# The gates of the recurrence as 64-row products on two halves of the array, two tiles at a time

## The chip, the core and the metric

The kernel runs on one core of one Trainium2 chip. Its time is the device time of one execution in microseconds (us); lower is better. Times are medians over executions, and a profile is one execution taken by the hardware profiler. Engines in it: PE (TensorE: matrix products; PEld is its weight load, shown apart), ACT (ScalarE: functions of one operand), DVE (VectorE: element work on two operands), POOL (GpSimd) and SP (SyncE, which here only issues DMAs). Products write into PSUM, eight banks of 128 partitions x 512 f32 elements; everything else is in SBUF or in device memory.

## What is computed

One layer of a decoder over 512 tokens of width 1024: a normalisation, one combined projection, three token mixers side by side (a gated chunk mixer, block-sparse attention, a recurrence), their gated sum, an output projection, and a SwiGLU block. The change lies in the recurrence:

```python
xc = lax.conv_general_dilated(xr, conv_w[:, None, :], window_strides=(1,), padding=[(CONV_WIDTH - 1, 0)],
                              dimension_numbers=('NWC', 'WIO', 'NWC'), feature_group_count=RNN_WIDTH) + conv_b
xh = xc.reshape(B, S, RNN_HEADS, RNN_HEAD_DIM)                       # 16 heads of 64
r = sigmoid(einsum('bshi,hio->bsho', xh, w_a).reshape(B, S, RNN_WIDTH) + b_a)
i = sigmoid(einsum('bshi,hio->bsho', xh, w_x).reshape(B, S, RNN_WIDTH) + b_x)
log_a = -LRU_C * r * softplus(-lam)
a = exp(log_a)
b_in = sqrt(-expm1(2.0 * log_a)) * (i * xc)
h_t = a_t * h_(t-1) + b_in_t                                         # over the 512 tokens
y_c = h * gelu(gate)
```

Each of the 16 heads has its own 64x64 matrix for each of the two gates, r and i.

## The kernel before

**Arithmetic.** Every f32 product is made of three in a faster form: an operand is split into a high part (an ACT copy, `hi`) and a low part (a DVE subtraction, `lo`) by `split` (L131, L136), and hi·hi, hi·lo and lo·hi are added up in one PSUM bank.

**Tiles.** Work goes by tiles of 128 output columns x 512 tokens. `matrix` (L269, products at L263) makes one with 24 products: eight blocks of the inner dimension, three each. Before it `unit` (L252) takes weights that are already split, and has the weights two tiles ahead loaded (SP) and split; loaded weights have two buffers, split ones three. In this stage PSUM has six banks for tag `mm` and two for tag `tr` (L72).

**The recurrence.** Its 1024 channels are eight tiles (`xr_tile`, L488), in two batches of four; a tile holds two heads, one on partitions 0 to 63, one on 64 to 127. A tile does this: 24 products; the convolution out of the bank (one ACT instruction, L499, and three DVE ones, L501) into `xc`; the split of `xc` into `ch` and `cl`; a pause; then the gates. For each gate there is a 128x128 weight matrix with the two heads' matrices on its diagonal and zeros elsewhere, three products of 128 rows (L509: hi·ch, hi·cl, lo·ch) into a bank of tag `tr`, and one ACT instruction that evicts it: a sigmoid into `R` (L511), or a tanh into `TI` (L514), which DVE multiplies by `xc` (L515). The gate weights are split early, during the first stage, by `load_wab` (L464).

`rec_batch` (L518) then takes a whole batch: tanh of `R` (L523), a square root of all four tiles (L524, for which ACT loads another table), exponentials (L530, yet another table), two DVE products and the scan over tokens. `rg_tile` (L545) makes the other factor, `rec_out` (L551) multiplies and splits the results, `yc_sums` (L567) forms sums of them (the first at L577) that the branch's products (L1273) read.

**Order.** Tiles are Python generators. `run` (L2049) walks through a list of them, one step at a time, a step being about six products. A tile that yields a number w is put on a list of late tiles and its remaining part is resumed after w steps of the tiles that follow, one part per step; what is left at the end of a pass is run out there. Beside the main list a side generator is advanced at a given rate per step. Three passes matter here: the first four `xr_tile`s and a small tile (`gate_tile`: 16 products, then four 64-row transposes, L722, of what a sigmoid at L718 gave); then four `rg_tile`s, a `cmp_tile` and the second four `xr_tile`s, with `rec_batch(0)` beside them at rate 0.45; then more tiles, with `both_out` (L2128: recurrence of batch 1, outputs of both) beside them, also at 0.45.

The order in which the code issues instructions is a priority. A planner with modelled costs then lays out each engine's queue at build time and draws a ready instruction ahead of an earlier one that it thinks is not ready; `issue_after` forbids that for a pair. On the chip every engine works through its queue in order and waits on semaphores.

Of the kernel before, what the change touches and what calls it, by code (L numbers as in the profile page):

```python
# [25 lines left out]
F32R = mybir.dt.float32r  # L26
I32 = mybir.dt.int32
AF = mybir.ActivationFunctionType
OP = mybir.AluOpType
# [4 lines left out]
NK = 8  # L34
# [9 lines left out]
V_CW, V_CB, V_BA, V_BX, V_LAM = 48, 80, 88, 96, 104  # L44
# [8 lines left out]
def hybrid_block(ctx: ExitStack, tc: tile.TileContext, A, out):  # L53
    nc = tc.nc
    V, SC, GP, PE, SY = nc.vector, nc.scalar, nc.gpsimd, nc.tensor, nc.sync
# [42 lines left out]
    def nm(s):  # L98
        cnt[0] += 1
        return f"{s}_{cnt[0]}"  # L100

    def slab(name, dt=F32, tag=None, shape=(4, S), first=0):
        pool, bufs = (merge if tag == "m" else big, TAGS[tag]) if tag in TAGS else phase_pool[tag]
        if tag not in ("y", "mo", "f", "wab"):
            return pool.tile([128, *shape], dt, tag=tag, name=nm(name), bufs=bufs)
        size = 2064 if tag == "f" else 2112
        t = pool.tile([128, size], dt, tag=tag, name=nm(name), bufs=bufs)[:, first:first + math.prod(shape)]
        return t if len(shape) == 1 else t.rearrange(
            "p (a b) -> p a b" if len(shape) == 2 else "p (a b c) -> p a b c", **dict(zip("abc", shape)))

    def row(name, dt=F32, tag="row", first=0):
        bufs = {"row": 6, "q32": 2, "tg": 2}[tag]
        return mid.tile([128, S if tag == "row" else S + 32], dt, tag=tag, name=nm(name), bufs=bufs)[:, first:first + S]

    def bank(tag):
        return psum[1].tile([128, S], F32, tag=tag, name=nm(tag), bufs=psum[2][tag])
# [10 lines left out]
    def f32(ap):  # L127
        return ap.bitcast(F32)

    def split(src, hi, lo, lo_eng=None):  # L130
        res["hi"] = SC.activation(hi, src, AF.Copy)  # L131
        e = lo_eng or V
        if e is GP:
            GP.tensor_sub(lo, src, f32(hi))
        else:
            res["lo"] = V.tensor_sub(lo, src, f32(hi))  # L136

    res = {}
# [138 lines left out]
    def const0(shape, name):  # L277
        return phase_pool["s0"][0].tile(shape, F32, name=name, bufs=1)
# [7 lines left out]
    vec = const0([128, NVEC], "vec")  # L286
# [3 lines left out]
    half = const0([128, 3, 8], "half")  # L290
# [164 lines left out]


    wab = {}

    def start_wab():
        wab["raw"] = slab("wabr", tag="s1", shape=(2, NK, 128))  # L460
# [2 lines left out]

    def load_wab():  # L464
        raw = wab["raw"]
        hi = slab("wabh", F32R, "wab", (2, NK, 128), 48)
        lo = slab("wabl", F32R, "wab", (2, NK, 128), 48)
        wab["hi"], wab["lo"] = hi, lo
        for _ in range(4):
            yield  # L470
        for k in range(0, NK, 2):
            split(raw[:, :, k:k + 2], hi[:, :, k:k + 2], lo[:, :, k:k + 2])
            yield

    yc = {}
    rec = {}
# [11 lines left out]
    def xr_tile(b, c):  # L488
        if c == 0:
            res["late"] = res["raw"]  # L490
            rec[b] = dict(R=slab("r", tag="y" if b else "m"), GG=slab("gg", tag="m"), TI=slab("ti", tag=("s0", "s1")[b]))
        k = 4 * b + c
        ps = bank("mm")
        yield from matrix(ps, hh, hl)
        xc = row("xc")

        def cw(w):
            return vec[:, V_CW + 8 * w + k:V_CW + 8 * w + k + 1]
        res["xc"] = SC.activation(xc, ps, AF.Identity, scale=cw(3), bias=vec[:, V_CB + k:V_CB + k + 1])  # L499
        for i in (1, 2, 3):  # L500
            res["cv"] = V.scalar_tensor_tensor(xc[:, i:], ps[:, :S - i], cw(3 - i), xc[:, i:], op0=OP.mult, op1=OP.add)  # L501
        yield
        ch, cl = row("ch", F32R), row("cl", F32R)
        split(xc, ch, cl)
        yield 4
        for g, dst in ((0, "R"), (1, "TI")):
            pg = bank("tr")
            for t, (w, x) in enumerate((("hi", ch), ("hi", cl), ("lo", ch))):
                PE.matmul(pg, wab[w][:, g, k, :], x, start=(t == 0), stop=(t == 2))  # L509
            if g == 0:  # L510
                SC.activation(rec[b]["R"][:, c, :], pg, AF.Sigmoid, bias=vec[:, V_BA + k:V_BA + k + 1])  # L511
            else:
                ti = rec[b]["TI"][:, c, :]
                last = SC.activation(ti, pg, AF.Tanh, scale=0.5, bias=half[:, 0, k:k + 1])  # L514
                res["ti"] = last, V.scalar_tensor_tensor(ti, ti, 1.0, xc, op0=OP.add, op1=OP.mult)  # L515
            yield

    def rec_batch(b):  # L518
        r = rec[b]
# [180 lines left out]
    gates = shared.tile([128, 4, 64], F32, name="gates")  # L700
# [6 lines left out]
    def gate_tile():  # L707
        ps = bank("mm")
        w, _ = unit()
        for k in range(NK):  # L710
            for t, x in enumerate((hh, hl)):
                PE.matmul(ps, w[:, k * 128:k * 128 + 128], x[k], start=(k == t == 0), stop=(k == NK - 1 and t == 1))
            if k % 4 == 3:
                yield
        s = row("gsig")
        SC.activation(s[:64], ps[64:], AF.Copy)
        V.tensor_add(s[:64], s[:64], ps[:64])
        SC.activation(s[:64], s[:64], AF.Sigmoid)  # L718
        yield
        pt = bank("tr")  # L720
        for c in range(4):
            PE.transpose(pt[:, c * 64:(c + 1) * 64], s[:64, c * 128:(c + 1) * 128], ident[:64, :64])  # L722
        V.tensor_copy(gates.rearrange("p c h -> p (c h)"), pt[:, :256])
        V.tensor_scalar(gates[:, 0, 0:48:3], gates[:, 0, 0:48:3], seen, None, op0=OP.mult)
        yield

    def cmp_tile(i):
        kv, pr = divmod(i, 2)
        if i == 0:
            x = slab("xcmp", tag="xc", shape=(2, G, 8, 32))  # L730
            comp[0], comp[1] = x[:, 0], x[:, 1]
        X = comp[kv]
        ps = bank("mm")
        yield from matrix(ps, *((gh, gl) if i == 0 else (hh, hl)))

        def half_of(x, g):
            return x[g * 64:(g + 1) * 64].rearrange("p (m r e) -> p m r e", r=8, e=2)

        src = [half_of(ps, g) for g in range(2)]
        dst = [X[:, 2 * pr + g].rearrange("p r m -> p m r") for g in range(2)]  # L740
        for g in range(2):
            if i == 0:
                r = half_of(rbs, g)
                V.tensor_mul(dst[g][0:64], src[g][:, :, :, 0], r[:, :, :, 0])
                V.tensor_mul(dst[g][64:128], src[g][:, :, :, 1], r[:, :, :, 1])
            else:
                res["x0"] = SC.activation(dst[g][0:64], src[g][:, :, :, 0], AF.Copy)
        if i:
            for g in range(2):
                V.tensor_copy(dst[g][64:128], src[g][:, :, :, 1])  # L750
        yield
# [1294 lines left out]
            close(0, 3, 2 - n, part)  # L2046


    def run(main, side=None, rate=1.0):  # L2049


        credit = 0.0
        late = []
        for m in main:
            for w in m:
                for x in late:
                    x[0] -= 1
                if late and late[0][0] <= 0:
                    if next(late[0][1], 0) == 0:
                        late.pop(0)  # L2060
                if w:
                    late.append([w, m])
                    break
                credit += rate
                while side is not None and credit >= 1.0:
                    credit -= 1.0
                    if next(side, 0) == 0:
                        side = None
            credit += rate
        for _, m in late:  # L2070
            for _ in m:
                pass
        if side is not None:
            for _ in side:
                pass

    def seq(*gens):
        for g in gens:
# [19 lines left out]
    def four(tile, b):  # L2098
        return [tile(b, c) for c in range(4)]
# [10 lines left out]
    def xr_tiles(b, nxt):  # L2110

        tiles = four(xr_tile, b) + [nxt]
        return tiles[:1] + [behind(t, "xc", "cv") for t in tiles[1:]]
# [4 lines left out]
    def branch(b, y, j0=0, j1=8):  # L2118
# [3 lines left out]
        return r  # L2122

    run([v_half(0), v_half(1), cmp_tile(0)], seq(norm(), load_wab()))
    run(xr_tiles(0, gate_tile()))
    tiles = xr_tiles(1, rg_tile(1, 0))
    run(four(rg_tile, 0) + [cmp_tile(1)] + tiles[:4], rec_batch(0), 0.45)
    def both_out():  # L2128

        batch = rec_batch(1)  # L2130
        next(batch)
        yield
        yield from after(res["ti"], rec_out(0))
        yield from batch
        yield from rec_out(1)

    def inputs(tile, kv):

        for w in tile:
# [4 lines left out]

    run([tiles[4], *(rg_tile(1, c) for c in range(1, 4)), cmp_tile(2), inputs(cmp_tile(3), 0),
         behind(c_gate(0), "x0", "x1"), hidden(first), inputs(c_gate(1), 1)],
        both_out(), 0.45)
    c_stage(first)
    run([u_tile(j) for j in range(8)])
    next_phase(1)  # L2150
# [115 lines left out]
```

## Time and profile before

| | |
|---|---|
| time, median of 3 (lowest to highest) | 1090.08 us (1089.75 to 1090.09) |
| the profiled execution: its time, its span | 1089.44 us, 1087.7 us |
| clock granted to PE in it | 0.998 of full |
| gate products (L509) | 48, in the stretch from 66.8 to 146.0 us |
| evictions of gates on ACT (L511 and L514) | 16, 0.68 us each |
| table loads on ACT between 50 and 215 us | 6, 1.28 us each |

How to read the views: the page gives busy time by engine as a share of the span, and the chain of work that ended last, followed back from the last instruction to what released it at each step. The same chain can be listed in order of time (start, length, engine, bank's tag, line, count). Groups of instructions are listed by line, with busy time and mean length of one, then the idle time of the engine before them and who ended it. The timeline lists instructions in order of time (start, length, engine, line, operation, output<-inputs, the array's rows*columns that a product uses, its shape, count; several merged instructions have one length in all). A product's own length is a latency: products are pipelined, and what one costs in a stream is the distance between two starts. The table by stretches gives, for each, the busy us (and number) of PE, PEld, DVE, ACT and POOL, then the granted clock, the DMA engines' busy share and GB/s.

### The profile page before, as it was taken

Reading aid. Unit: us, or ns where it says so; the run is one execution under the profiler, and the core shown is the slowest. Engines: PE = TensorE matmul, PEld = TensorE weight load, DVE = VectorE, ACT = ScalarE, POOL = GpSimd, SP = SyncE. Lnnn points to the kernel's source line nnn. Section 1 sums busy time; section 2 is a strip of 40 time slices with the busy share of each in tenths; the row PEclk is TensorE's granted clock in tenths of the full one; section 3 lists DMA queues with packets and bytes.
Section 4 is the critical chain, followed back from the end, with each engine's and each line's share of the span. In section 5 each row is a group of like instructions: output and inputs, shape, how many; then the busy total and the mean of one; then the engine's idle time right before and its main releaser. Section 6 shows DMA issues by size and latency. Waiting matters only on the chain.

```text
span 1087.7 us, 16765 instructions
## 1 busy us (share of the span) xinstructions
PE 1078.3 (99%) x6450; PEld 948.5 (87%) x6450; DVE 883.0 (81%) x1557; ACT 661.7 (61%) x1210; POOL 29.0 (3%) x41
## 2 busy tenths in 40 slices
PE   9999999999999999999999999999999999999997
PEld 7888888999889888898888889988999999998886
DVE  6967779669675899998998887876988888889675
ACT  6757574454444676876777655555666666667542
POOL 0000000000000000000000000000000000022200
PEclk9999999999999999999999999999999999999999
DMA  8332325430322221102111134271323322378902
GB/s 312 113 99 82 97 86 204 178 98 20 117 78 78 78 59 39 59 20 79 59 39 59 58 118 136 72 257 39 117 78 117 117 104 97 130 227 202 191 20 97
DMA packets 35312, 115.07 MB, mean 106 GB/s; under 512 B 3584, under 2 KB 3984, under 8 KB 34336
## 3 DMA queue, kind: packets, MB, share of 16 engines
q1 hardware_dynamic: 28496, 97.01, 27.0%
q0 software_dynamic: 5152, 11.09, 5.0%
q10 hardware_dynamic: 1584, 5.90, 1.4%
q8 instruction: 50, 0.82, 0.3%
q14 instruction: 30, 0.25, 0.1%
HBM read 111.89 MB, written 2.10 MB: 105 GB/s over the span
## 4 chain that ended last, share of the span: by engine, by line
PE 97%; DVE 1%; DMA 0%; issue 0%; ACT 0%; DVEq 0%; SPq 0%; ACTq 0%
PE mm L263 37%; PE mm L1755 18%; PE mm L1273 7%; PE mm L1894 6%; PE mm L625 4%; PE mm L1509 4%; PE o L992 4%; PE sc L954 3%; PE tr L979 3%; PE tr L1894 3%; PE mm L870 2%; PE tr L784 1%; PE tr L509 1%; PE mm L1611 1%; PE tr L685 1%; PE tr L892 1%
## 5 line engine op out<-in xcount | busy, mean ns | idle before, releaser
L263 PE MATMUL mm<-hh,hi 128*128 128x512 f32 x504 | 199.5, 396 | 0.0
L263 PE MATMUL mm<-hh,lo 128*128 128x512 f32 x504 | 197.4, 392 | 0.0
L263 PE MATMUL mm<-hl,hi 128*128 128x512 f32 x504 | 196.9, 391 | 0.0
L136 DVE TENSOR_TENSOR lo<-raw,hi 128x1024 fp32r<-128x1024 f32 (+1 forms) x105 | 121.0, 1153 | 38.4 <-ACT hi L131 35.3
L131 ACT ACTIVATE hi<-raw 128x1024 fp32r<-128x1024 f32 (+1 forms) x105 | 105.3, 1003 | 46.5 <-PE mm L263 17.3
L263 PEld LDWEIGHTS mm<-hh,lo 128*128 128x128 f32 x504 | 94.6, 188 | 19.7
L263 PEld LDWEIGHTS mm<-hl,hi 128*128 128x128 f32 x504 | 94.7, 188 | 18.4 <-issue 0.2
L263 PEld LDWEIGHTS mm<-hh,hi 128*128 128x128 f32 x504 | 94.7, 188 | 18.0 <-PE mm L1273 0.2
L960 ACT ACTIVATE P<-P,ast 128x128 f32<-128x128 f32 (+3 forms) x128 | 70.7, 555 | 23.1 <-DVE ast L958 22.5
L958 DVE CUSTOM_DVE_ANT_0 P<-sc,mask 128x128 f32<-128x128 f32 (+3 forms) x128 | 57.9, 484 | 8.2 <-PE sc L954 7.3
L131 ACT ACTIVATE ph<-tr 128x512 fp32r<-128x512 f32 x80 | 46.9, 592 | 25.9 <-PE tr L979 24.0
L136 DVE TENSOR_TENSOR pl<-tr,ph 128x512 fp32r<-128x512 f32 x80 | 54.4, 685 | 2.7 <-PE o L992 0.9
L954 PE MATMUL sc<-K,q 128*128 128x512 f32 (+2 forms) x192 | 51.0, 368 | 0.0
L1755 PE MATMUL mm<-t,hi 128*128 128x256 f32 x288 | 50.7, 276 | 0.0
L1894 PE MATMUL mm<-hi,u 128*128 128x512 f32 x160 | 50.1, 389 | 0.0
L979 PE MATMUL tr<-ident,P 128*128 128x128 f32 x320 | 48.7, 273 | 0.0
L979 PEld LDWEIGHTS tr<-ident,P 128*128 128x128 f32 x320 | 39.0, 140 | 9.8 <-DVE pl L136 1.0
L136 DVE TENSOR_TENSOR lo<-bs,hi 128x1024 fp32r<-128x1024 f32 x28 | 34.1, 1220 | 11.6 <-ACT hi L131 11.6
L1755 PEld LDWEIGHTS mm<-t,hi 128*128 128x128 f32 x288 | 43.4, 188 | 0.0
L1755 PE MATMUL mm<-fh,hi 128*128 128x256 f32 x144 | 40.0, 278 | 0.0
L1755 PE MATMUL mm<-fh,lo 128*128 128x256 f32 x144 | 39.8, 276 | 0.0
L1755 PE MATMUL mm<-fl,hi 128*128 128x256 f32 x144 | 39.8, 276 | 0.0
(489 smaller groups left out, 2896.6 us busy)
## 6 DMA issues: line engine op xcount, KB each, us to landing
raw<-in_w_in SPq DMA_DIRECT2D x64, 512.0 KB, 3.5
rawp<-in_w_fi SPq DMA_DIRECT2D x20, 1024.0 KB, 5.1
bs<-in_w_fo POOLq DMA_DIRECT2D x20, 512.0 KB, 8.1
raw<-in_w_br SPq DMA_DIRECT2D x14, 512.0 KB, 3.6
w<-in_cw ACTq DMA_DIRECT2D x4, 1024.0 KB, 6.7
raw<-in_w_o SPq DMA_DIRECT2D x8, 512.0 KB, 4.1
bs<-in_w_fo SPq DMA_DIRECT2D x8, 512.0 KB, 8.0
raw<-in_w_v SPq DMA_DIRECT2D x6, 512.0 KB, 4.9
```

The lines of the kernel that those rows point to most:

```text
L131: res["hi"] = SC.activation(hi, src, AF.Copy)
L136: res["lo"] = V.tensor_sub(lo, src, f32(hi))
L263: res["mm"] = PE.matmul(ps[:m, n0:n1], w[:, k * 128:k * 128 + m], x[k][:, n0:n1], start=(t == 0), stop=(t == 3 * NK - 1))
L625: res["mm"] = PE.matmul(b[c], x[k][:, c * 128:(c + 1) * 128], w[:, kk * 512:kk * 512 + 512], start=(k == 0 and t == 0), stop=(k == NK - 1 ...
L954: PE.matmul(ps[:, :w * n].rearrange("p (b n) -> p b n", b=w), lhs, K[:, i, brs[0]:brs[-1] + 1, :n], start=(i == 0), stop=(i == 1))
L958: V.tensor_tensor_reduce(out=t, in0=ps[:, b * n:b * n + n], in1=mask[0][:, S - n:], scale=-0.125, scalar=3.0e38, op0=OP.add, op1=OP.min, a ...
L960: SC.activation(t, t, AF.Exp, scale=-1.0, bias=st[:, 0, j, b:b + 1], accum_out=st[:, 1, j, b:b + 1])
L979: PE.transpose(pt[:, j * 128:(j + 1) * 128], self.part(j, br)[:, kt * 128:(kt + 1) * 128], ident)
L992: PE.matmul(po, VV[:, kt, g % 2, br].rearrange("p i d -> p (i d)"), x, start=(br == 0 and kt == 0 and t == 0), stop=(br == 1 and kt == a a ...
L1273: res["mm"] = PE.matmul(ps, u[:, k * 128:k * 128 + 128], v[:, k], start=(start and k == t == 0), stop=(k == 3 and t == 2), skip_group_chec ...
L1755: res["mm"] = PE.matmul(ps, w[:, k * 128:k * 128 + 128], x[:, k], start=(start and k == t == 0), stop=(k == 3 and t == 2), skip_group_chec ...
L1894: PE.matmul(ps, a, b, start=id(ps) not in begun, stop=i == len(ops) - 1, skip_group_check=True)
```

## The change

- The gate weights are laid out by head: each half of the partitions holds its head's 64 rows, with the two gates' 64 columns side by side (`load_wab`).
- A tile's gate work is no longer done alone. The even tile of a pair is only noted; when the odd one's pause has passed, both are done as a group: four banks of tag `mm` (one for each tile and head), and twelve products of 64 rows and 128 columns, alternating between the two halves, in the order hi·ch, lo·ch, hi·cl, the odd tile ahead of the even one in each. All but the first are tied to the one before by `issue_after`.
- A bank now holds one head's two gates, the first on its partitions 0 to 63, the second on 64 to 127. So each tile has four evictions of 64 partitions instead of two of 128.
- `ch` and `cl` use the buffers of tags `tg` and `q32` (two each) instead of `row` (six).
- The pause is 3 steps instead of 4, and for the last tile of a batch 6 (batch 0) or 4 (batch 1). `run` can hand its list of late tiles on to the next pass (`keep`, `late`), so each batch's second group falls into the pass behind it. The side generators wait, a step at a time, until the batch's two groups are laid out.

```diff
-        hi = slab("wabh", F32R, "wab", (2, NK, 128), 48)
-        lo = slab("wabl", F32R, "wab", (2, NK, 128), 48)
+        hi = slab("wabh", F32R, "wab", (NK, 128), 48)
+        lo = slab("wabl", F32R, "wab", (NK, 128), 48)
...
-        for k in range(0, NK, 2):
-            split(raw[:, :, k:k + 2], hi[:, :, k:k + 2], lo[:, :, k:k + 2])
-            yield
+        for o in ends:
+            for i in range(2):
+                g = slice(64 * i, 64 * i + 64)
+                split(raw[o, i, :, o], hi[o, :, g], lo[o, :, g])
+                yield
...
-        ch, cl = row("ch", F32R), row("cl", F32R)
+        ch, cl = row("ch", F32R, "tg"), row("cl", F32R, "q32")
         split(xc, ch, cl)
-        yield 4
-        for g, dst in ((0, "R"), (1, "TI")):
-            pg = bank("tr")
-            for t, (w, x) in enumerate((("hi", ch), ("hi", cl), ("lo", ch))):
-                PE.matmul(pg, wab[w][:, g, k, :], x, start=(t == 0), stop=(t == 2))
-            if g == 0:
-                SC.activation(rec[b]["R"][:, c, :], pg, AF.Sigmoid, bias=vec[:, V_BA + k:V_BA + k + 1])
-            else:
-                ti = rec[b]["TI"][:, c, :]
-                last = SC.activation(ti, pg, AF.Tanh, scale=0.5, bias=half[:, 0, k:k + 1])
-                res["ti"] = last, V.scalar_tensor_tensor(ti, ti, 1.0, xc, op0=OP.add, op1=OP.mult)
-            yield
+        rec[b]["x"] = rec[b].get("x", []) + [(k, xc, ch, cl)]
+        yield (6 - 2 * b) if c == 3 else 3
+        if c % 2 == 0:
+            return
+        two = rec[b].pop("x")
+        pg = [[bank("mm") for _ in ends] for _ in two]
+        for t in range(3):
+            for i, (k, xc, ch, cl) in reversed([*enumerate(two)]):
+                w, x = (("hi", ch), ("lo", ch), ("hi", cl))[t]
+                for n, own in enumerate(ends):
+                    with tc.issue_after(res["gate"].ins) if t or n or not i else nullcontext():
+                        res["gate"] = PE.matmul(pg[i][n], wab[w][own, k, :], x[own], start=(t == 0), stop=(t == 2))
+        yield
+        for i, (k, xc, ch, cl) in enumerate(two):
+            R, ti = (rec[b][n][:, k % 4, :] for n in ("R", "TI"))
+            for n, own in enumerate(ends):
+                SC.activation(R[own], pg[i][n][:64], AF.Sigmoid, bias=vec[own, V_BA + k:V_BA + k + 1])
+                last = SC.activation(ti[own], pg[i][n][64:], AF.Tanh, scale=0.5, bias=half[own, 0, k:k + 1])
+            res["ti"] = last, V.scalar_tensor_tensor(ti, ti, 1.0, xc, op0=OP.add, op1=OP.mult)
+            yield
+        rec[b]["gates"] += 1
...
-    def run(main, side=None, rate=1.0):
+    def run(main, side=None, rate=1.0, late=None, keep=False):
...
-    run(xr_tiles(0, gate_tile()))
+    late = run(xr_tiles(0, gate_tile()), keep=True)
...
+    def gated(b):
+        while rec[b]["gates"] < 2:
+            yield
+        yield from rec_batch(b)
+
+    late = run(four(rg_tile, 0) + [cmp_tile(1)] + tiles[:4], gated(0), 0.45, late, True)
     def both_out():
+        while rec[1]["gates"] < 2:
+            yield
         batch = rec_batch(1)
```

`ends` is `slice(0, 64), slice(64, 128)`; `rec[b]["gates"]` starts at 0.

More of the change, by code (lines that the diff above doesn't have):

```diff
@@ L457, in hybrid_block @@
     wab = {}
+    ends = slice(0, 64), slice(64, 128)
     def start_wab():
@@ L490, in xr_tile @@
             res["late"] = res["raw"]
-            rec[b] = dict(R=slab("r", tag="y" if b else "m"), GG=slab("gg", tag="m"), TI=slab("ti", tag=("s0", "s1")[b]))
+            rec[b] = dict(gates=0, R=slab("r", tag="y" if b else "m"), GG=slab("gg", tag="m"), TI=slab("ti", tag=("s0", "s1")[b]))
         k = 4 * b + c
@@ L2046, in down @@
             close(0, 3, 2 - n, part)
-    def run(main, side=None, rate=1.0):
+    def run(main, side=None, rate=1.0, late=None, keep=False):
         credit = 0.0
-        late = []
+        late = late or []
         for m in main:
@@ L2069, in run @@
             credit += rate
-        for _, m in late:
-            for _ in m:
+        while late and not keep:
+            for _ in late.pop(0)[1]:
                 pass
@@ L2075, in run @@
                 pass
+        return late
     def seq(*gens):
@@ L2124, in hybrid_block @@
     run([v_half(0), v_half(1), cmp_tile(0)], seq(norm(), load_wab()))
-    run(xr_tiles(0, gate_tile()))
+    late = run(xr_tiles(0, gate_tile()), keep=True)
     tiles = xr_tiles(1, rg_tile(1, 0))
-    run(four(rg_tile, 0) + [cmp_tile(1)] + tiles[:4], rec_batch(0), 0.45)
+    def gated(b):
[3 more added lines that the diff above has]
+    late = run(four(rg_tile, 0) + [cmp_tile(1)] + tiles[:4], gated(0), 0.45, late, True)
     def both_out():
+        while rec[1]["gates"] < 2:
+            yield
         batch = rec_batch(1)
@@ L2146, in hybrid_block @@
          behind(c_gate(0), "x0", "x1"), hidden(first), inputs(c_gate(1), 1)],
-        both_out(), 0.45)
+        both_out(), 0.45, late)
     c_stage(first)
```

## The prediction

> **What bounds the kernel now.** I read the page first: span, busy time by engine, the chain that ended last.
>
> ```profile
> span 1087.7 us, 16765 instructions
> PE 1078.3 (99%) x6450; PEld 948.5 (87%) x6450; DVE 883.0 (81%) x1557; ACT 661.7 (61%) x1210; POOL 29.0 (3%) x41
> PE 97%; DVE 1%; DMA 0%; issue 0%; ACT 0%; DVEq 0%; SPq 0%; ACTq 0%
> ```
>
> PE is busy 99% of the span and holds 97% of the chain. A busy PE is not a PE at its peak, so next come the chain in order of time and what PE's weight loads waited for between 50 and 215 us, where the changed work lies.
>
> ```profile
> 50.61 16.32 PE mm L263 x72
> 66.93 1.36 PE tr L509 x6
> 68.29 5.44 PE mm L263 x24
> 73.73 1.36 PE tr L509 x6
> ...
> 145.13 0.91 PE tr L509 x4
> ```
>
> ```profile
> PEld tr L722 <- ACT gsig L718: 0.4, 1, 0.4
> PEld tr L509 <- ACT ch L131: 0.2, 1, 0.2
> PEld tr L784 <- issue: 0.2, 1, 0.2
> ```
>
> 72 products in 16.32 us are 0.2267 us each; the six gate products (L509) in 1.36 us keep the same 0.2267, and PE passes from one kind to the other without a gap. In all this stretch it waits 0.8 us. So PE's stream is the time here, and what the change takes out of it goes to the end, unless PE then meets a wait that it did not meet before.
>
> **The change part by part.** The gate products first.
>
> ```profile
> L509 PE MATMUL tr<-ch,wabh x16: 389/389/496, 66.8 to 143.6; 128*128 128x512 f32 x16
> L509 PE MATMUL tr<-cl,wabh x16: 389/389/389, 67.0 to 145.4; 128*128 128x512 f32 x16
> L509 PE MATMUL tr<-ch,wabl x16: 389/389/389, 67.2 to 145.7; 128*128 128x512 f32 x16
> ```
>
> These are 48 products of 128 rows, each half zeros (two heads on a block diagonal). 389 ns is a latency; at 0.2267 us apart they take 48 x 0.2267 = 10.88 us, or 2.72 us for the twelve of two tiles. After the change two tiles again take twelve products, 64 rows deep and 128 columns wide: each head's product now gives both gates. Each neighbouring pair sits on different halves of the array and writes different banks. If the halves run at the same time, two tiles take six steps of 0.2267 = 1.36 us.
>
> Changing between 128 and 64 rows costs something. The trace has one such place, four 64-row transposes, here with their line and PE's timeline around them:
>
> ```profile
> L722 PEld LDWEIGHTS tr<-ident,gsig x4: 135/138/138, 87.7 to 87.9; 64*128 64x128 f32 x4
> L722 PE MATMUL tr<-ident,gsig x4: 221/222/272, 87.7 to 87.9; 64*128 64x64 f32 x4
> 87.39 0.39 PE L263 MATMUL mm<-hh,hi 128*128 128x512 f32 x1
> 87.71 0.46 PE L722 MATMUL tr<-ident,gsig 64*128 64x64 f32 x4
> 88.10 0.50 PE L509 MATMUL tr<-ch,wabh 128*128 128x512 f32 x1
> 88.43 0.39 PE L509 MATMUL tr<-cl,wabh 128*128 128x512 f32 x1
> ```
>
> Going in: the product at 87.39 leaves room at 87.62; the first transpose has 272 instead of 222 ns, so it really starts at about 87.71 + 0.05 = 87.76, 0.14 us late, and part of that may be its wait for the sigmoid. Coming out: the last transpose starts at 88.17 - 0.22 = 87.95, and at the spacing of the four, (87.95 - 87.76)/3 = 0.063 us, the next could start at 88.01; since the one behind it starts at 88.43, the product at 88.10 really starts at 88.43 - 0.227 = 88.20, 0.19 us late. In and out make 0.33 us. The ends are 0, if 512-column products hide the change, and 0.6 (twice the 0.3 gap from 88.10 to 88.43). I take 0.33, the measured pair.
>
> One group of two tiles then costs 1.36 + 0.33 = 1.69 instead of 2.72 us, a gain of 1.03; four groups gain **4.1 us**. With the ends of the switch cost the gain is 5.4 or 3.0.
>
> That the halves overlap is shown by no row: the four transposes all lie on one half. From below a pair costs 0.2267 (full overlap); from above 0.4535 (none). The row nearest to it is the spacing of 0.063 us: a 64-row product with weights of its own is issued, loaded and streamed in that time, so neither issue (two in 0.126) nor weight loads fill the 0.2267 that a pair has. I take the lower end. [...]
>
> Does a group stand waiting in front of PE? It is issued after 18 products of the following tile in the first group of each batch, 18 x 0.2267 = 4.08 us after the odd tile's own last product, and needs ch at once, cl only after four pairs. The first tile's rows show how long these take:
>
> ```profile
> 61.58 0.78 ACT L499 ACTIVATE xc<-mm,vec 128x512 f32<-128x512 f32 x1 [4.66 <-PE mm L263]
> 64.81 0.63 ACT L131 ACTIVATE ch<-xc 128x512 fp32r<-128x512 f32 x1 [1.49 <-DVE xc L501]
> 65.76 0.69 DVE L136 TENSOR_TENSOR cl<-xc,ch 128x512 fp32r<-128x512 f32 x1
> ```
>
> From the start of xc, ch ends 3.86 us and cl 4.87 us later; the group starts at 4.08 and asks for cl at 4.08 + 0.14 + 4 x 0.227 = 5.13. Both are there, by 0.2 to 0.3 us: I cost it at nothing, and 0.3 per group of this kind (0.6 in all) if the cover goes. The second groups are issued 28 or 30 products after their tile, over 6 us, and have time. A wait there would hold all of PE's queue, the following tile's products first.
>
> ACT gets more to do: 64-row evictions take as long as 128-row ones, and there are 32 instead of 16.
>
> ```profile
> L511 ACT ACTIVATE r<-tr,vec 128x512 f32<-128x512 f32 x8 | 5.5, 684 | 3.9 <-PE tr L509 3.9
> L718 ACT ACTIVATE gsig<-gsig 64x512 f32<-64x512 f32 x1 | 0.6, 618 | 0.0
> 66.90:95.00 28.10, 28.10 (x127) 23.01 (x126) 16.48 (x23) 21.36 (x28) 0.00 (x0) 1.00 0.30 93
> 125.50:146.10 20.60, 20.60 (x92) 16.89 (x91) 13.84 (x18) 13.91 (x20) 0.00 (x0) 1.00 0.29 85
> 146.10:180.00 33.90, 33.90 (x152) 28.09 (x151) 30.10 (x43) 23.28 (x35) 0.00 (x0) 1.00 0.43 150
> ```
>
> Sixteen more at about 0.6 are 9.6 us, in four blocks of eight (4.8 us). ACT is free 6.7 us in each of the first two windows and 10.6 in the third, so PE's stream covers them. Behind a block wait the split of the next weights (prepared two tiles, 10.9 us, ahead) and the next tile's convolution. Banks: a group holds four of six, the running tile one, and the sixth serves the next tile for 5.4 us, by when two evictions (1.2 us) have freed the first. The weights' split (four ACT and four DVE instructions of 512 elements) keeps count and length; DVE's work and the DMAs are the same. The move of ch and cl to other buffers costs nothing: with two of each, a tile's pair is used up before the tile after next needs it.
>
> Carrying the second groups into the next pass starts each batch's recurrence later. For batch 1: its tiles end 3 x 1.03 = 3.1 us earlier; the last tile's own products end at 139.14 in the rows below, and the last group ends 30 products and 1.69 us after that, at 139.14 - 3.1 + 6.8 + 1.7 = 144.5, against 146.04 before. But eight evictions follow instead of two, and two tanh: the square root can begin its table load at about 150 to 151 instead of 148.47, 2 to 3 us later. Whether PE notices is read at the end of that chain:
>
> ```profile
> 139.14 1.36 PE tr L509 x6
> 146.04 34.00 PE mm L263 x150
> 148.47 1.28 ACT L524 ACT_TABLE_LOAD   x1
> 184.94 1.29 DVE L136 TENSOR_TENSOR ycl<-ti,ych 128x512 fp32r<-128x512 f32 x2
> 189.98 1.22 DVE L577 TENSOR_TENSOR ti<-ti 128x1024 f32<-128x1024 f32 x1
> 205.34 1.22 DVE L136 TENSOR_TENSOR t<-ti,t 128x1024 fp32r<-128x1024 f32 x1 [1.97 <-ACT t L131]
> 211.48 9.57 PE mm L1273 x84
> ```
>
> The recurrence's last output is split at 186.2; the sums (L577) begin at 189.98, 3.8 us later; their first split is ready at 206.56, while the product that reads it is the 28th of the 84, at 211.48 + 27 x 0.114 = 214.6, 8.0 us later. Slack: 11.8 us. The change uses 2.5 of it plus the 4.1 by which PE comes sooner, 6.6. I cost the delay at nothing.
>
> Sum: -4.1 us. The profiled execution took 1089.44 us (its span is 1087.7), 0.06% below the median of 1090.08. From 1089.44 it comes to 1085.3, from the median to **1086.0**.
>
> **Rivals.**
>
> [...] 14%; groups that the planner breaks up with 128-row products, at 0.33 a break (eight breaks are 2.6 us, gain 1.5), are counted here, since they give the same time and the change then does only half of what it says.
>
> *The halves do not overlap (the slower side).* Place: the four groups. Price: 12 x 0.2267 + 0.33 = 3.05 a group, 0.33 more than now, so +1.3 us: 1091.4. It decides as soon as a pair costs over (2.72 - 0.33)/6 = 0.40 us. If each product also showed a load of 0.138, the group would be 4.7 and the kernel 1098. Nothing in the profile speaks against it but the short spacing of L722, which shows issue and loads, not two halves. 13%, of it 4% beyond 1092.3.
>
> *The late recurrence.* The second side stream is held until the last group's evictions are laid out, four of its steps, about seven steps of the main stream at 1.36 = 9.5 us. If its instructions keep that distance, the chain uses 9.5 + 4.1 = 13.6 of 11.8 us and PE waits 1.8 at L1273: gain 2.3, 1087.8. DVE is 89% busy from 146 to 180 (30.10 of 33.90), which speaks for it; that the planner now draws such steps forward into idle time speaks against. 7%; each further us of queueing there would cost one more.
>
> **How the numbers follow.** Forecast 66% (1084.7 to 1087.1), loads or breaks 14% (1088.6), no overlap 13% (1091.4), late recurrence 7%. The range reaches from 1084.6, a switch that costs nothing, to 1089.2, past the second case, leaving out about 18%. A difference of 0.2%, 2.2 us, is about what can be told from no change. Faster by more: the forecast, a quarter of the second case and 2% of the last, 71%. Slower by more: 4% of the third and 1% of the last, 5%. Within: 24%.
>
> **What would show it.** Right: the gate products in four runs of twelve, form 64*128, pairs with nearly equal starts, pairs 0.23 us apart, 0.1 to 0.2 us lost at each end; ACT with 32 evictions of 0.6 us; L1273 beginning about 4 us sooner with no wait ahead of it. Wrong: starts evenly 0.23 us apart (no overlap) or pairs 0.34 apart (loads); 128*128 products between them; PE's loads waiting for ch, cl or t.

## The result: 0.5% slower, and the profile after

| | before | after |
|---|---|---|
| time, median of six runs each (lowest to highest), us | 1089.76 (1089.41 to 1090.09) | 1095.57 (1093.75 to 1096.27) |
| the profiled execution: its time, its span, us | 1089.44, 1087.7 | 1095.61, 1093.9 |

The ratio is 1.0051, with a 95% interval of 1.0039 to 1.0064. The forecast was 1086.0, the range ended at 1089.2: the time lies 6.4 us above it. Of two of the kernels further down one execution each ran at a mean granted clock of 0.56 and 0.75, and their medians leave it out. The page of the changed kernel:

```profile
PE 1079.2 (99%) x6450; PEld 946.0 (86%) x6450; DVE 885.1 (81%) x1557; ACT 676.6 (62%) x1226; POOL 29.3 (3%) x41
...
PE 86%; DVE 6%; ACT 5%; DMA 1%; issue 1%; DVEq 0%; ACTq 0%
```

PE's busy time is as before, but PE's share of the chain that ended last fell from 97% to 86%: DVE, ACT and DMA now hold parts of it, so PE waits somewhere. The waits of PE's weight loads between 45 and 300 us (who waited for whom: us in all, times, longest):

```profile
PEld tr L796 <- DVE x L777: 3.7, 1, 3.7
...
PEld mm L519 <- ACT ch L131: 1.3, 2, 0.9
...
PEld tr L734 <- ACT gsig L730: 1.1, 1, 1.1
```

The largest stands at a place that the prediction does not name: L796 is the first product of the compression (`cmp_tile`, L784 of before), and it waits for DVE's `x` (L777, which is L765 of before): the input of the compression, plus a position term.

**The products do what they were meant to.** PE's timeline around the first group:

```profile
70.67 0.39 PE L263 MATMUL mm<-hh,lo 128*128 128x512 f32 x1
70.99 0.74 PE L519 MATMUL mm<-ch,wabh 64*128 64x512 f32 x4
71.56 0.63 PE L519 MATMUL mm<-ch,wabl 64*128 64x512 f32 x4
72.02 0.64 PE L519 MATMUL mm<-cl,wabh 64*128 64x512 f32 x4
72.59 0.50 PE L263 MATMUL mm<-hh,hi 128*128 128x512 f32 x1
72.93 0.40 PE L263 MATMUL mm<-hl,hi 128*128 128x512 f32 x1
```

Four products, two pairs, lie 72.02 - 71.56 = 0.46 us apart: 0.23 a pair, full overlap. The switch: PE has room at 70.67 + 0.227 = 70.90; the first four take 0.57 where the next four take 0.46, so the first really starts near 71.10, 0.20 late. The last four end at 72.02 + 0.46 = 72.48, and the first wide product, going by the one behind it, starts at 72.93 - 0.227 = 72.70, 0.22 late. A group takes 72.70 - 70.90 = 1.80 us, 0.92 less than the 2.72 of before; four gain 3.7. The second group is not in one piece: the gate tile's transposes (L734, L722 of before) stand in it and wait for their sigmoid.

**Where it is lost.** The place before the change, in the timeline (DVE's last scan of batch 1, then `x`; PE's first product of the compression):

```profile
174.59 1.22 DVE L542 TENSOR_TENSOR_SCAN ti<-r,t 128x512 f32<-128x512 f32 x1
176.31 1.21 DVE L765 TENSOR_TENSOR x<-xcmp,cpe 128x1024 f32<-128x1024 f32 x1
179.88 1.38 PE L784 MATMUL tr<-x,w 128*128 128x124 f32 x11
```

The same after the change:

```profile
180.99 1.22 DVE L554 TENSOR_TENSOR_SCAN ti<-r,t 128x512 f32<-128x512 f32 x1
182.70 1.22 DVE L777 TENSOR_TENSOR x<-xcmp,cpe 128x1024 f32<-128x1024 f32 x1
183.98 0.79 PE L796 MATMUL tr<-x,w 128*128 128x124 f32 x2 [3.30 <-DVE x L777]
```

`x` uses no number of the recurrence. But its slab has the tag of the buffer in which `rec_batch` keeps T, so it can be written only when the last scan has read T:

```python
        r["T"] = slab("t", tag="s2")
...
        X = [slab("x1", tag="s2", shape=(G, 8, 32)), comp[kv]]
```

Before, `x` was there at 176.31 + 1.21 = 177.52, and PE came at 179.88: 2.4 us of slack. The last scan now comes 6.4 us later. Why the chain ahead of it is late is seen on ACT:

```profile
147.54 0.67 ACT L524 ACTIVATE r<-mm,vec 64x512 f32<-64x512 f32 x1
...
152.47 0.69 ACT L525 ACTIVATE ti<-mm,half 64x512 f32<-64x512 f32 x1
153.18 0.60 ACT L451 ACTIVATE gs<-mm 128x512 f32<-128x512 f32 x1
153.80 1.06 ACT L131 ACTIVATE hi<-raw 128x1024 fp32r<-128x1024 f32 x1
154.77 0.71 ACT L535 ACTIVATE t<-r,sp 128x512 f32<-128x512 f32 x1
...
157.12 1.28 ACT L536 ACT_TABLE_LOAD   x1
```

The last group's eight evictions take 153.16 - 147.54 = 5.6 us, 0.70 each. Then the square of a gelu and a weight split come ahead of the tanh instructions, and the table load starts at 157.12, 8.65 us later than before (148.47).

The rest comes behind the wait. First stretches of the changed kernel behind 180.4 us, then lines of both kernels, some of PE's timeline and some of the chain.

```profile
180.40:184.00 3.60, 0.30 (x3) 0.03 (x1) 3.60 (x6) 2.21 (x3) 0.00 (x0) 0.95 0.00 0
184.00:188.00 4.00, 4.00 (x23) 4.00 (x23) 4.00 (x5) 0.00 (x0) 0.72 (x1) 0.62 0.19 18
188.00:192.60 4.60, 4.60 (x44) 4.60 (x43) 2.43 (x4) 0.63 (x1) 0.00 (x0) 1.00 0.77 242
```

Before:

```profile
186.94 0.48 PE L263 MATMUL mm<-hh,hi 128*128 128x512 f32 x1
...
221.05 5.46 PE mm L263 x24
```

After:

```profile
192.61 0.48 PE L263 MATMUL mm<-hl,hi 128*128 128x512 f32 x1
...
218.76 6.30 DMA raw<-in_w_in
...
226.23 1.24 DVE lo L136
226.25 0.50 PE L263 MATMUL mm<-hh,hi 128*128 128x512 f32 x1 [0.49 <-ACT hi L131]
```

PE is busy 0.30 of 3.60 us, and for the next 4 us the granted clock is 0.62: 64 compression products take 8.63 us (183.98 to 192.61) instead of 7.06 (179.88 to 186.94). Then the first branch products (L1285, L1273 of before) and the wait behind them take from 214.05 to 226.25, 12.2 us instead of 9.57: PE's weight loads wait 1.5 us in them, 1.3 of it for ACT, and the next tile's first load another 0.7 for the split of its weights. That tile then takes 6.4 instead of 5.46. Its weights were loaded at 218.76 only, behind the last instruction that read their buffer, a split that began at 217.52; the split that the tile's second wait is for ends at 227.47.

| from before to after | us |
|---|---|
| ahead of the compression (groups -3.7; new waits and order in and around them +1.4) | -2.3 |
| the wait for `x`, 180.5 to 183.98 | +3.5 |
| the compression at a lower clock, 8.63 - 7.06 | +1.6 |
| the first branch products and the wait behind them, 12.2 - 9.57 | +2.6 |
| the tile behind them, waiting for its weights | +1.0 |
| sum, before rounding; the spans differ by 6.2 | +6.3 |

The first row goes by equal work: 13 more products (L263) stand ahead of the compression than before; PE's stream ends at 180.52, and 180.52 - 13 x 0.227 = 177.57, against 179.88. Of the 1.4 us in it PE's idle time shows 1.2: 0.5 for `ch` and 0.7 for the gate tile's sigmoid. The wait can be counted from the other side: 6.4 (scan later) - 2.4 (slack) + 2.3 (PE sooner) - 2.95 (13 products drawn ahead) = 3.35, against 3.30 in the row.

### The profile page after: what moved, and what is told of

It reads as the page before. It is cut to its first block, busy times and chain, and to the rows that moved or that the text cites. A ratio compares the mean times of both kernels' runs of the same rounds, so it can differ in the third digit from the quotient of the medians.

```text
span 1093.9 us, 16795 instructions
## 1 busy us (share of the span) xinstructions
PE 1079.2 (99%) x6450; PEld 946.0 (86%) x6450; DVE 885.1 (81%) x1557; ACT 676.6 (62%) x1226; POOL 29.3 (3%) x41
## 4 chain that ended last, share of the span: by engine, by line
PE 86%; DVE 6%; ACT 5%; DMA 1%; issue 1%; DVEq 0%; ACTq 0%
PE mm L263 28%; PE mm L1767 17%; PE mm L1906 6%; PE mm L1285 6%; PE mm L637 4%; PE mm L1521 4%; PE o L1004 4%; PE sc L966 3%; PE tr L991 3%; PE tr L1906 3%; PE mm L882 2%; DMA raw<-in_w_in 1%; DVE lo L136 1%; PE mm L1623 1%; ACT ti L525 1%
## 5 line engine op out<-in xcount | busy, mean ns | idle before, releaser
L263 PE MATMUL mm<-hh,hi 128*128 128x512 f32 x504 | 200.0, 397 | 0.5 <-ACT hi L131 0.5
L263 PE MATMUL mm<-hh,lo 128*128 128x512 f32 x504 | 197.6, 392 | 0.5 <-DVE lo L136 0.5
L263 PE MATMUL mm<-hl,hi 128*128 128x512 f32 x504 | 197.1, 391 | 0.0
L131 ACT ACTIVATE hi<-raw 128x1024 fp32r<-128x1024 f32 (+1 forms) x105 | 105.4, 1005 | 46.1 <-PE mm L263 12.2
L263 PEld LDWEIGHTS mm<-hh,lo 128*128 128x128 f32 x504 | 94.6, 188 | 20.7 <-DVE lo L136 1.2
L263 PEld LDWEIGHTS mm<-hh,hi 128*128 128x128 f32 x504 | 94.7, 188 | 20.1 <-issue 1.5
L263 PEld LDWEIGHTS mm<-hl,hi 128*128 128x128 f32 x504 | 94.7, 188 | 18.2 <-issue 0.2
```

Of the source, the lines that this page charges most:

```text
L263: res["mm"] = PE.matmul(ps[:m, n0:n1], w[:, k * 128:k * 128 + m], x[k][:, n0:n1], start=(t == 0), stop=(t == 3 * NK - 1))
```

## The experiments

A is the theory above: the carried groups and the evictions make batch 1's recurrence late, and T's buffer hands the delay to the compression. The rivals lay the loss elsewhere: B in the sixteen more evictions on ACT, wherever the groups stand, C in a queue of DVE that is simply full. Each run is set against runs of the kernel before on the same chip: medians 1090.21 (the first four), 1089.85 (the next four) and 1089.74 us (the last four).

**A buffer of its own for T** (`e1_t_own`, the changed kernel with batch 1's T in another slab):

```diff
-        r["T"] = slab("t", tag="s2")
+        r["T"] = slab("t", tag="y" if b else "s2")
```

> The changed kernel, but the tile T of batch 1's recurrence lies in a free buffer of tag y instead of s2, so that the compression's input x, which takes s2 next, need not wait for the last scan. Theory A (the carried group and the held side stream start batch 1's recurrence some 8 us late, its square root's table load at 157.1 instead of 148.5, and that reaches PE through the buffer s2): the wait of 3.3 us ahead of the compression's products goes and PE reaches them about 2 us sooner than before the change; 4 to 5 us come back, 1089.5 to 1092. Theory C (DVE's queue is simply full there, the buffer is not the link): x stays at its place behind the last scan, the wait stays over 2.5 us, 1094 to 1096.

1091.80 us (1091.1 to 1092.52), ratio 1.0014 (1.0005 to 1.0024): 1.6 us above the kernel before instead of 5.8, in A's range. PE's timeline at the compression, and at the third group:

```profile
131.87 0.50 PE L519 MATMUL mm<-ch,wabh 64*128 64x512 f32 x2 [3.04 <-ACT ch L131]
...
181.91 1.27 PE L796 MATMUL tr<-x,w 128*128 128x124 f32 x10
```

No wait is left at L796, nor in the branch products. But PE comes to the compression at 181.91, not some 2 us sooner than before (179.88), because a new wait of 3.04 us stands ahead of the third group. DVE shows why:

```profile
122.30 1.22 DVE L777 TENSOR_TENSOR x<-xcmp,cpe 128x1024 f32<-128x1024 f32 x1
123.55 1.22 DVE L777 TENSOR_TENSOR xcmp<-xcmp,cpe 128x1024 f32<-128x1024 f32 x1
124.81 2.32 DVE L504 SCALAR_TENSOR_TENSOR xc<-mm,vec,xc 128x511 f32<-128x511 f32 x3
```

With its buffer free, the planner drew `x` forward by over 50 us and put it ahead of the convolution for which `ch`, and so the group, waits. So it was the buffer that held `x`, and not a full queue: C falls. But the experiment freed one thing and moved another, and behind the new wait the granted clock was 0.50 to 0.52 from 133 to 136 us.

**Batch 1's second group not carried** (`e2_b1_not_carried`):

```diff
-    late = run(four(rg_tile, 0) + [cmp_tile(1)] + tiles[:4], gated(0), 0.45, late, True)
+    late = run(four(rg_tile, 0) + [cmp_tile(1)] + tiles[:4], gated(0), 0.45, late)
```

> The changed kernel, but batch 1's second group is laid out at the end of its own pass and not carried into the next. Theory A: the table load for batch 1's square root comes at 149 to 152 us, PE waits under 1 us ahead of the compression, and the time is 1086 to 1090. Theory B (the sixteen more evictions on ACT, 0.70 us apart, are what is late, wherever the group stands): the load at 155 or later, a wait of over 2.5 us, 1093 to 1096.

1095.48 us (1094.59 to 1095.82), 1.0049 (1.0034 to 1.0064). The table load comes at 153.78 and PE's weight loads wait 0.7 us at the compression, so the late recurrence is largely undone, and yet no time is won: A's number missed, and where the other number fits, its reason does not. PE now waits for `ch` ahead of the last group:

```profile
143.19 1.22 PE L519 MATMUL mm<-ch,wabh 64*128 64x512 f32 x4 [5.62 <-ACT ch L131]
144.21 1.05 PE L519 MATMUL mm<-ch,wabl 64*128 64x512 f32 x4
```

```profile
137.00:143.00 6.00, 0.57 (x3) 0.15 (x1) 5.36 (x7) 5.32 (x8) 0.00 (x0) 0.87 0.29 78
143.00:146.00 3.00, 2.81 (x12) 1.81 (x12) 1.15 (x2) 0.14 (x1) 0.00 (x0) 0.50 0.48 141
```

The group stands next in PE's queue while ACT and DVE still make its operands; and then the clock is 0.50, and the first four products take 1.02 us instead of 0.57. Carrying has this use: it keeps other products in front of the group.

**None carried** (`e3_none_carried`, the first pass as well):

```diff
-    late = run(xr_tiles(0, gate_tile()), keep=True)
+    late = run(xr_tiles(0, gate_tile()))
```

> The changed kernel with neither batch's second group carried. Theory A: like the kernel that carries batch 0's alone, within 1.5 us of it, as batch 0's recurrence has slack; the 1.1 us that PE waits for the gate tile's sigmoid may go or stay. Theory B: 1093 to 1096 here as well.

1097.02 us (1096.54 to 1097.26), 1.0063 (1.0048 to 1.0078), outside both ranges, though only just outside A's 1.5 us above `e2_b1_not_carried` (1.54). The wait for `ch` is there again, 5.61 us at 145.10, and a new one of 2.01 us stands ahead of the second group.

**Only the carrying** (`e4_carry_alone`, the kernel before with its 128-row products and 16 evictions, late lists and gated side generators of the change, and these pauses):

```diff
-        yield 4
+        yield ((6 - 2 * b) if c == 3 else 4)
```

> The kernel before with its gates tile by tile as 128-row products in tag tr and sixteen evictions, with only the carrying added: the last tile's gates of each batch 6 and 4 steps later, in the next pass, and the side streams held until the batch's gates are laid out. Theory A: batch 1's recurrence is late (table load at 152 or later), PE waits ahead of the compression by 1.5 us or more, and the kernel is slower than before by 2 to 7 us: 1092 to 1097. Theory B: as before, 1089.3 to 1090.5.

1092.63 us (1091.39 to 1093.14), 1.0021 (1.0011 to 1.003), so +2.4 us. Its timeline of ACT, DVE and PE:

```profile
150.15 1.28 ACT L525 ACT_TABLE_LOAD   x1
...
178.88 1.23 DVE L543 TENSOR_TENSOR_SCAN ti<-r,t 128x512 f32<-128x512 f32 x1
...
181.88 0.82 PE L785 MATMUL tr<-x,w 128*128 128x124 f32 x5 [1.80 <-DVE x L766]
```

The time fits A. The load is only 1.7 us late, less than A said, but the last scan is 4.3 us late, and the same wait appears: 4.3 - 2.4 = 1.9, and 1.80 is seen. The clock stayed at 1.00 behind it in this execution.

**Only the evictions** (`e5_evictions_alone`, the kernel before, each of the 16 evictions in two of 64 partitions):

```diff
-                SC.activation(rec[b]["R"][:, c, :], pg, AF.Sigmoid, bias=vec[:, V_BA + k:V_BA + k + 1])
+                for own in (slice(0, 64), slice(64, 128)):
+                    SC.activation(rec[b]["R"][own, c, :], pg[own], AF.Sigmoid, bias=vec[own, V_BA + k:V_BA + k + 1])
```

(the tanh likewise)

> The kernel before, with each of its sixteen gate evictions split into two of 64 partitions; products, banks and order of the groups stay. Theory A (sixteen more evictions alone are covered; it takes the carrying, which is worth 2.4 us by itself): 1089.5 to 1091, batch 1's square root within 1.5 us of 148.5. Theory B (the evictions are what makes it late): the table load 3 us or more later, PE waiting ahead of the compression, 1091.5 to 1094.

1092.09 us (1091.38 to 1092.65), 1.0015 (1.0006 to 1.0025): +2.2 us, in B's range, where A had foreseen next to nothing. The timeline:

```profile
149.91 1.28 ACT L526 ACT_TABLE_LOAD   x1
...
177.59 1.22 DVE L544 TENSOR_TENSOR_SCAN ti<-r,t 128x512 f32<-128x512 f32 x1
...
179.42 0.63 ACT L131 ACTIVATE ych<-ti 128x512 fp32r<-128x512 f32 x1 [4.82 <-DVE ti L560]
...
181.38 1.24 DVE L752 COPY xcmp<-mm 64x256 f32<-64x256 f32 x2 [0.26 <-ACT xcmp L749]
...
183.94 0.82 PE L786 MATMUL tr<-xcmp,w 128*128 128x124 f32 x5 [1.29 <-DVE xcmp L767]
```

The load is only 1.4 us late, which A had right, but the last scan 3.0 us; then PE waits 1.29 us inside the compression and 0.87 us in the first branch products. The recurrence is late here too, but this wait is not for the buffer of T: `x` is there at 180.52, just before PE comes at 180.66. PE waits for the second input, `xcmp` (L767). In DVE's queue it stands behind two copies that wait for ACT, and ACT had waited 4.82 us for the recurrence's output. A late recurrence thus reaches the compression through the queues of ACT and DVE as well. Carrying alone makes the scan 4.3 us late, evictions alone 3.0, the change 6.4, and the slack of 2.4 is there only once.

**T's own buffer, with `x` held in place** (`e8_t_own_x_held`, the mended kernel from here on: on top of `e1_t_own`, both inputs of the compression are held behind `res["cv"]`, the last convolution):

```diff
-            with tc.issue_after(res["hid"][1].ins) if kv else nullcontext():
+            with tc.issue_after((res["hid"][1] if kv else res["cv"]).ins):
```

> The changed kernel with T of batch 1 in a buffer of tag y, and the two DVE additions that make the compression's input held behind the last tile's convolution, so that they aren't drawn in front of an earlier tile's. Theory A: no wait ahead of the compression and none of 3 us for ch; what the gate groups save on PE (3.7 us, less about 1.5 for the waits for the gate tile's sigmoid and for one ch) stays: 1087 to 1088.5. If something else made the changed kernel slow: 1090 or more.

**1087.33 us** (1086.66 to 1088.79), ratio 0.9974 (0.9963 to 0.9985): 2.5 us under the kernel before, where the changed one is 5.8 us above it. Run again beside the last three experiments it gave 1087.38 us, 0.998 (0.997 to 0.9989). Its timeline at the compression:

```profile
156.63 1.28 ACT L536 ACT_TABLE_LOAD   x1
...
177.57 1.16 PE L796 MATMUL tr<-x,w 128*128 128x124 f32 x9
...
181.94 1.22 DVE L554 TENSOR_TENSOR_SCAN ti<-r,t 128x512 f32<-128x512 f32 x1
```

The recurrence is as late as in the changed kernel (table load at 156.63 against 157.12, last scan at 181.94 against 180.99), and the compression does not wait: `x` is made at 144.39, and PE reaches the compression at 177.57, the 2.3 us sooner of the table. So in the changed kernel the delay costs time through the place of `x` behind the last scan, which the buffer gave it, and not by itself. In this kernel's profiled execution, the longest of its seven (1088.79 us), PE waits 1.45 us for ACT at 218.83: the eviction that it waits for stands in ACT's queue behind a weight split, and that had waited 2.35 us for its DMA.

**The gate tile's transposes later** (`e9_transposes_late`, on top of the mended kernel):

```diff
         SC.activation(s[:64], s[:64], AF.Sigmoid)
-        yield
+        yield 4
```

> The same, and the gate tile's four 64-row transposes come four steps later, so that no product of the second group stands behind them and their wait for the sigmoid. Theory A: PE's wait for the sigmoid (1.1 us) goes, the transposes need a change to 64 rows of their own (0.33): 0.5 to 0.9 us under the kernel without this edit. If the wait was covered: no difference.

1092.93 us (1090.58 to 1095.4), 1.0025 (1.0015 to 1.0035): 5.6 us above the mended kernel, where 0.5 to 0.9 us below it was expected. The sigmoid's wait went, but PE's timeline has two others:

```profile
109.21 0.50 PE L263 MATMUL mm<-hh,lo 128*128 128x512 f32 x1 [1.23 <-DVE lo L136]
...
327.45 0.50 PE L263 MATMUL mm<-hh,hi 128*128 128x512 f32 x1 [3.27 <-DVE u L454]
```

The second lies 230 us behind the edit. That one moved step gave the planner another order for all that follows is the likely reason, but no run shows it.

**The halves one after the other** (`e11_no_overlap`, the mended kernel with six products of one half, then six of the other):

```diff
-        for t in range(3):
-            for i, (k, xc, ch, cl) in reversed([*enumerate(two)]):
-                w, x = (("hi", ch), ("lo", ch), ("hi", cl))[t]
-                for n, own in enumerate(ends):
+        for n, own in enumerate(ends):
+            for t in range(3):
+                for i, (k, xc, ch, cl) in reversed([*enumerate(two)]):
+                    w, x = (("hi", ch), ("lo", ch), ("hi", cl))[t]
```

> As with T in its own buffer and x held, but the products of a group are issued one half of the array after the other, six and six, so that neighbours never lie on different halves except at one place. If two halves run together only when neighbours alternate: a group takes about 2.8 instead of 1.8 us, and the kernel is 3.5 to 4.6 us slower than the one with alternating halves, 1091 to 1092.5. If the order makes no difference: the same time.

1089.13 us (1088.38 to 1090.14), 0.9991 (0.9982 to 1.0001): 1.8 us more than the mended kernel, about half of the 3.5 to 4.6 that was expected without overlap. PE's timeline:

```profile
70.55 0.73 PE L519 MATMUL mm<-ch,wabh 64*128 64x512 f32 x2
...
71.22 0.50 PE L519 MATMUL mm<-ch,wabh 64*128 64x512 f32 x1
71.35 0.39 PE L519 MATMUL mm<-ch,wabl 64*128 64x512 f32 x1
...
72.81 0.50 PE L263 MATMUL mm<-hh,hi 128*128 128x512 f32 x1
```

A group takes 72.81 - 70.55 = 2.26 us, against 1.60 between the same rows of the changed kernel (72.59 - 70.99). The `wabh` product at 71.22 is already the second half's first, and a product of the first half (71.35) starts behind it: the halves overlap even where the order keeps them apart. So this run does not take the overlap away, only a part of it.

**The buffers alone** (`e12_before_t_own`, the kernel before with the two edits of the mended one):

> The kernel before, gates unchanged, with only T of batch 1 in a buffer of tag y and the compression's input held behind the last convolution. Theory A (PE did not wait there before, so a free buffer brings nothing by itself): 1089 to 1091. If the buffers alone are what makes the mended kernel fast: 1087 to 1088.

1090.16 us (1089.39 to 1091.33), 1.0004 (0.9994 to 1.0013): nothing, as expected. The slack is worth nothing to a kernel that doesn't use it, so the mended kernel's gain is the change's own.

**All but the 64-row products** (`e13_rows128_mended`: the carrying, the split evictions and the mended buffers, with 128-row products):

> Carrying, sixteen more evictions (each gate in two halves) and the buffers of the mended kernel, but products of 128 rows: only the 64-row products are missing. Theory A: with the buffer free, carrying and evictions cost little, and the difference to the mended kernel is what the products save on PE, four groups of 2.72 against 1.8 less 1.5 us of new waits: 1089.5 to 1091.5, 2 to 4 us above the mended kernel. If the products save nothing: as fast as the mended kernel, 1087 to 1088.

1090.34 us (1089.1 to 1090.75), 1.0004 (0.9995 to 1.0014), with no wait at the compression. Beside it the mended kernel took 1087.38: the 64-row products, in their groups of two tiles, save 3.0 us of time, out of 3.7 us in PE's stream. The rest agrees with what PE waits more in the mended kernel's profile around the groups: 0.5 us for `ch` and 0.2 for the sigmoid.

**Longer pauses ahead of the groups** (`e14_groups_later`, the mended kernel with one step more ahead of the first groups and two more ahead of batch 0's second):

```diff
-        yield (6 - 2 * b) if c == 3 else 3
+        yield (8 - 4 * b) if c == 3 else 4
```

> The mended kernel with each group one step later (pauses of 4, and 8 and 4 for the last tiles of the batches), so that the odd tile's ch is ready and the gate tile's transposes are out of the second group. Theory A: the waits for ch (0.5) and for the sigmoid (up to 1.1) go from the groups: 1086 to 1087. If a later recurrence shows again, or the planner's later order changes: 1088 or more.

1088.58 us (1087.97 to 1090.27), 0.9992 (0.9983 to 1.0002): a miss, with the time of the other case; no run shows which of its reasons holds. It was to take away PE's waits for `ch` (0.5 us) and for the sigmoid (0.7 us), and both grew, to 1.45 and 1.13 us:

```profile
132.30 0.73 PE L519 MATMUL mm<-ch,wabh 64*128 64x512 f32 x4 [1.45 <-ACT ch L131]
```

## Why the prediction was wrong

- **The products: right, a little too large.** Pairs 0.23 us apart, as forecast. The switch measured 0.20 + 0.22 = 0.42 instead of 0.33, a group 1.80 instead of 1.69, the gain 3.7 instead of 4.1. No run shows weight loads that add to a pair, on which the rival at 1088.6 us stands (0.34 a pair): the pairs lie 0.23 us apart, and with that no overlap (0.4535) falls too.
- **"I cost the delay at nothing": the step that failed.** The slack of 11.8 us was worked out along the data, to the sums at L577 and the product at L1273. The first to wait was an instruction that reads nothing of the recurrence and only takes over T's buffer; to it the slack was 2.4 us. `e8_t_own_x_held` shows it: with that tie cut, and `x` held at a harmless place, an equally late recurrence costs nothing at the compression.
- **The size of the delay: too small.** The table load was to be 2 to 3 us later; it was 8.65, and the last scan 6.4. Eight evictions lie 0.70 apart, not 0.6, and the planner put a gelu's square and a weight split ahead of the tanh. The last group also ended no sooner than before, at 145.63 + 0.46 = 146.1 instead of 144.5, and its evictions began 1.4 us after that. The right slack with the predicted 2 to 3 us would still have shown a wait: 2.5 + 2.3 (PE sooner) is more than 2.4.
- **"PE's stream covers" 16 more evictions: wrong.** Free time of ACT in a window is a mean; the last block of eight stands in the chain to the scan. By themselves these evictions cost 2.2 us (`e5_evictions_alone`).
- **Do the groups wait for `ch`?** Forecast at nothing, 0.3 each if the cover goes. In the changed kernel 1.3 us of weight-load waits, and in the variants 3.0 and 5.6: the cover hung on how DVE's queue was laid out, which the first tile alone doesn't show.
- **The late recurrence as a rival** had the right mechanism at the wrong place (1.8 us at L1273), and 7%. What the wait drew behind it, 1.6 us of lower clock and 3.6 us of late branch operands and weights, was in no case. That PE goes on at full clock behind a wait was assumed without being said.

What stays open: why, in `e2_b1_not_carried` and `e3_none_carried`, the planner did not draw the next tile's products ahead of the waiting group; the 1.4 us of new waits and order around the groups were read from the trace, but no run took them away without a new loss; and that the 3.6 us in the branch and the tile behind it follow from the wait for `x` is argued: with that wait gone, `e1_t_own` has no such wait there, but the mended kernel's longest execution has one.

## What to carry to other kernels

Work out the slack of a delayed chain to every reader behind it, and count as a reader whoever takes over a buffer that the chain holds: look up what else has the same tag. A free share of an engine in a window covers added work only if no chain with little slack runs through it. And where a buffer is freed, a planner may draw the released work forward in front of something more urgent, so free it and hold the work in place at once.

## What the runs showed of the hardware

- The granted clock fell behind some gaps in PE's work. After a wait of 3.3 us in the changed kernel the granted clock was 0.62 over the next 4 us (0.50 over the first three of them) and 1.00 from 188 us on; after 5.6 us in `e2_b1_not_carried` it was 0.50 over the next 3 us. Not every gap of about 3 us brought it: behind 3.04 us in `e1_t_own` it was 0.50 to 0.52 from 133 to 136 us (mean of that execution 0.996), behind 3.27 us in `e9_transposes_late` it stayed at 1.00 (mean 0.999, products 0.23 us apart). In the changed kernel the wait cost 1.6 us more than its length. Of its six executions five had a mean clock of 0.995 to 0.998 and took 1095.3 to 1096.27 us; the one at 0.999 took 1093.75.
- Evictions of 64 partitions took as long as those of 128 (0.67 to 0.69 us against 0.68), so packing two gates into one bank doubled ACT's work on them.
- Products of the second half started ahead of products of the first half that are before them in the program (71.22 against 71.35 in `e11_no_overlap`). The part ahead of the prediction says that every engine works through its queue in order; for PE's products that is not strictly so.
- Going from 128 to 64 rows and back cost PE 0.20 and 0.22 us at the first group.
